# Gate jobs of a two-layer trunk: the eight wide products grouped ahead of the eight narrow ones

## The chip, the cores and the metric

The kernel runs on one core of one Trainium2 chip. A core has a matrix engine, TensorE (PE in the profile; its weight loads are the row PEld), and VectorE (DVE), ScalarE (ACT), GpSimd (POOL) and SyncE (SP, which here only starts transfers). Each works through its own queue in the order in which the program wrote its instructions, and waits on semaphores for the others. The metric is the device time of one launch in microseconds, as the median of several runs; lower is better.

## The reference

The model is a decoder trunk over 512 tokens of width 1024 with two layers, all in float32. Layer 0 is a gated short convolution, layer 1 a sliding-window attention with sinks. Behind each stands the same feed-forward block, with F = 2816, and this block is what the change touches:

```python
def swiglu(h, w_gate_up, w_down):
    g, u = jnp.split(h @ w_gate_up, 2, axis=-1)
    return (jax.nn.silu(g) * u) @ w_down

ff = swiglu(rmsnorm(h, ffn_pre_norm[l]), ffn_w_gate_up[l], ffn_w_down[l])
h = h + rmsnorm(ff, ffn_post_norm[l])
```

## The kernel before

**Split products.** TensorE multiplies a reduced form of float32 (`fp32r`) here, so each factor is split into a high part and a low rest: ScalarE copies the high part (`whi`, L469 for weights), VectorE subtracts it from the full value (`wlo`, L470). A product is then three products, low by high, high by high and high by low; `mm3` (L190 to L193) issues these three into one accumulator.

**Seven products instead of eight.** The columns of the gate and up matrices beyond the first two pairs of blocks are done in groups. A group `q` (0 to 9 in each layer, so 20 in all) takes a 2 by 2 arrangement of weight blocks and of token blocks and forms seven block products, p = 1 to 7, from sums of weight blocks and of token blocks, in place of eight plain ones. Token sums are made once per layer (`factors`, L364), weight sums by accumulating transfers that GpSimd starts (L538) or by VectorE (L457).

**One gate job per product.** `gate_jobs` (L976) makes seven jobs per group in the order p = 1, 2, 6, 5, 7, 3, 4. Jobs 1, 6, 7 and 4 accumulate into chain X, two PSUM tiles `gx` (one for each e = 0, 1); jobs 5 and 3 into chain Z (`gz`), job 2 into chain Y (`gy`). Each job has e = 0, 1 and k = 0 to 3, so eight steps. Jobs 1, 2, 3 and 5 call `mm3` in each step: three products with 256 moving columns, 24 per job. For p = 6, 7 and 4 the token factor lies in one tile with its high and low halves, and a view of it with two stretches of 256 columns (`two[:, :, c:c+256]`, L387) is moved at once. So each step of jobs 6, 7 and 4 is one wide product of 512 columns, `whi` by both halves into the whole tile `gx` (L1048), and one narrow product of 256 columns, `wlo` by the high half into the first 256 columns of the same tile (L1050). There are 3 x 20 = 60 such jobs, and in each the wide and narrow products alternate: wide, narrow, wide, narrow, sixteen in all. In all three jobs the tile is already open, job 1 having started it.

**What follows a job.** `take(p)` (L1001) moves partial sums out of PSUM directly behind each job: for p = 6 and 4 a ScalarE copy (L1024) and a VectorE addition (L1008) for e = 0, then the same for e = 1; for p = 7 two VectorE additions for each e. The next X job may write `gx` only when these have read it; between two X jobs always lies a Y or Z job, except between job 4 of one group and job 1 of the next, which has other tiles.

**The order of work.** The code is under `tc.manual_schedule`: the order on each engine is the order in which the Python code emits instructions. `in_line` (L474) walks over the jobs of a layer: it emits a job's products, then the split of the weights for the job three places ahead (L500), further transfers and pending late steps. Between groups stand the down jobs, which multiply the gated activations by the down matrix with 512 moving columns (`seven`, L604, and `mm3`, tiles `px`, `py`, `pz`). A job's `whi` and `wlo` come from four buffers each, so the split for the job three ahead reuses the buffer of the job just before the current one.

Of the kernel before, what the change touches and what calls it, by code (L numbers as in the profile page):

```python
# [16 lines left out]
P = 128  # L17
D = 1024
S = 512
# [53 lines left out]
def yoco_kernel(  # L73
# [22 lines left out]
    nc = tc.nc  # L96
# [19 lines left out]
    def slot(s, dt=F32, w=S):  # L116
        return big.tile([P, w], dt, tag="slot", name=name(s), padded_shape=[P, S])

    def wide(s, dt=F32):
        return wides.tile([P, D], dt, tag="wide", name=name(s))  # L120
# [7 lines left out]
    def bank(s, pool=None):  # L128

        if pool is None:  # L130
            pool = (ps_mm, ps_sc, ps_mm, ps_pt)[turn[0] % 4]
            turn[0] += 1
        return pool.tile([P, S], F32, tag="bank", name=name(s))
# [56 lines left out]
    def mm3(out, whi, wlo, xhi, xlo, start, stop, **kw):  # L190
        nc.tensor.matmul(out, whi, xlo, start=start, stop=False, **kw)  # L191
        nc.tensor.matmul(out, whi, xhi, start=False, stop=False, **kw)  # L192
        nc.tensor.matmul(out, wlo, xhi, start=False, stop=stop, **kw)  # L193
# [354 lines left out]
    for l in range(2):  # L548
# [3 lines left out]
        for rd, (f0, f1) in enumerate(ROUNDS[:-1]):  # L552
            k = slice(f0 // 2, f1 // 2)
# [106 lines left out]
    with tc.manual_schedule(engines=ALL):  # L660
# [25 lines left out]
        for k in range(KT):  # L686
# [7 lines left out]
            for i in range(3):  # L694
                for t in range(3):
                    n = 3 * k + t
                    whi, wlo = (w[:, n % KT * P : (n % KT + 1) * P] for w in ws[n // KT])
                    nc.tensor.matmul(begun[0][t], (whi, wlo, whi)[i], xs[k][i == 2],
                                     start=k == i == 0, stop=k == KT - 1 and i == 2)
# [255 lines left out]
    def ffn(l, before, ahead, gain, gpres, following):  # L955
# [20 lines left out]
        def gate_jobs(q, factors, out, to, then):  # L976

            sums = sums_of[f"g{l}{q}"]  # L980
            a21, a22, a11, a12 = (Raw(b) for b in sums.blocks)
            s1, s3, *rest = (Raw(b) for b in sums.sums)
            raws = {1: [a11], 2: [a12], 5: [s1], 7: [s3], 4: [a22]}
            if rest:
                raws[6], raws[3] = ([r] for r in rest)
            else:
                raws[6], raws[3] = [a11, s1], [a12, a11]
            chain = {1: "X", 6: "X", 7: "X", 4: "X", 5: "Z", 3: "Z", 2: "Y"}
            pools = {"X": ps_mm, "Y": ps_pt, "Z": ps_sc}
            split = {}  # L990
            if q == 0:

                pools = {"X": ps_sc, "Y": ps_pt, "Z": ps_mm}
                raws[1], raws[2] = [], []
                split = {1: ahead.ready[4], 2: ahead.ready[5]}
            banks, kept = {}, []

            def tiles(a):
                return a.rearrange("p (e c) -> p e c", e=2)

            def take(p):  # L1001
                x, y, z = (banks.get(c) for c in "XYZ")
                st, u, gr = kept
                g0, g1 = (gr.rearrange("p (e h c) -> p e h c", e=2, h=2)[:, :, h]
                          for h in range(2))

                def add(out, a, b):
                    nc.vector.tensor_tensor(out=out, in0=a, in1=b, op=ALU.add)  # L1008

                if p == 2:  # L1010
                    add(g0, tiles(y), tiles(st))
                elif p == 5:
                    nc.scalar.activation(u, z, AF.Copy)
                elif p == 3:
                    add(g1, tiles(z), tiles(st))
                else:
                    for e in range(2):
                        a, b = x[e][:, :256], x[e][:, 256:]
                        ste, ue = (v[:, e * 256 : (e + 1) * 256] for v in (st, u))
                        if p == 7:  # L1020
                            add(ue, a, ue)
                            add(ue, b, ue)
                            continue
                        nc.scalar.activation(ste, a, AF.Copy)  # L1024
                        if p != 1:
                            add(ste, b, ste)
                if p == 4:
                    for g, m in ((g0, st), (g1, u)):
                        nc.vector.scalar_tensor_tensor(out=g, in0=tiles(m), scalar=-1.0, in1=g,
                                                       op0=ALU.mult, op1=ALU.mult)  # L1030

            def run(p):
                def products(job):
                    if not kept:
                        kept.extend([slot("st"), slot("st"), wide("gr")])
                    whi, wlo = split[p] if p in split else job.w
                    c = chain[p]
                    opened = c not in banks
                    if opened:
                        banks[c] = ([bank("gx", pools[c]) for _ in range(2)] if c == "X"  # L1040
                                    else bank("g" + c.lower(), pools[c]))
                    for e in range(2):
                        for k in range(4):
                            kk = slice(e * S + k * P, e * S + (k + 1) * P)
                            xhi, xlo, *xboth = factors[p][k]
                            kw = {"skip_group_check": True}
                            if c == "X" and xboth:
                                nc.tensor.matmul(banks[c][e], whi[:, kk], xboth[0], start=False,  # L1048
                                                 stop=False, **kw)
                                nc.tensor.matmul(banks[c][e][:, :256], wlo[:, kk], xhi,  # L1050
                                                 start=False, stop=k == 3 and p == 4, **kw)
                                continue
                            out = (banks[c][e][:, :256] if c == "X"
                                   else banks[c][:, e * 256 : (e + 1) * 256])
                            mm3(out, whi[:, kk], wlo[:, kk], xhi, xlo,
                                opened and k == 0 and (c == "X" or e == 0),
                                e == 1 and k == 3 and p in (2, 3), **kw)
                    take(p)
                return products

            def gate():
                nc.scalar.activation(kept[2], kept[2], AF.Silu)  # L1062

            def end():
                late = out(kept[2], to)
                then()
                return late

            return [Job(raws[p], run(p), {3: gate, 4: end}.get(p), len(raws[p]) > 1)
                    for p in (1, 2, 6, 5, 7, 3, 4)]  # L1070
# [42 lines left out]
        with tc.manual_schedule(engines=ALL):  # L1113
# [5 lines left out]
            def then(hf, k):  # L1119
                if hf == 0 and k in (5, 6):  # L1120
                    for b in ((0, 1), (2, 3))[k - 5]:
                        before.turn(b, (2,))
                if hf == 0 and k == 6:
                    for b in range(4):
                        before.turn(b, (3,))
                    for f in range(KT):
                        before.split(0, f, 1)
                    for b in range(4):
                        before.keep(b, 1)
                if hf == 1 and k == 1:  # L1130
                    factors.update(before.factors())
                if hf == 1 and k == 3:
                    sum_on(f"{l}f0")

            factors = {}
# [137 lines left out]
    class Heads:  # L1273
# [114 lines left out]
        def out(self):  # L1388
            hi, lo = slot("ohi", F32R), slot("olo", F32R)
            nc.scalar.activation(hi, self.po, AF.Copy)  # L1390
            nc.vector.tensor_tensor(out=lo, in0=self.po, in1=hi.bitcast(F32), op=ALU.subtract)
            at.append((hi, lo))
# [25 lines left out]
    with tc.manual_schedule(engines=ALL):  # L1418
        last_tile(res, [[(0, 4)], [(0, 5)], [], [(0, 6), (0, 7), (1, 0), (1, 1)],
                        [(1, f) for f in (4, 5, 2, 3, 6, 7)]])  # L1420
        for hf in range(2):
            c = slice(hf * 256, (hf + 1) * 256)
            for k in range(KT):
                kk = slice(k * P, (k + 1) * P)
# [192 lines left out]
```

## Time and profile before

| quantity | value |
|---|---|
| median of 3 runs | 1027.26 us (1026.03 to 1027.35) |
| time of the profiled execution | 1026.46 us |
| its span, first to last instruction | 1024.7 us |
| TensorE busy / weight loads busy | 1015.1 us / 900.3 us |
| VectorE / ScalarE / GpSimd busy | 858.7 / 582.3 / 196.9 us |
| granted TensorE clock | 0.999 |
| wide products of the 60 jobs (L1048) | 480, mean 399 ns |
| narrow products of the 60 jobs (L1050) | 480, mean 281 ns |

Products are pipelined: the duration of one is longer than the distance from its start to the start of the next, and durations overlap. What a sequence of products costs is therefore read from start times in the timeline, not from durations. The two feed-forward blocks' gate and down jobs run from 203.9 us to 470.9 us and from 709.3 us to 975.9 us of the span.

### The profile page before, as it was taken

The page shows a single profiled execution, that of the slowest core. Times are in us where ns is not written, and L with a number is a line of the kernel's source. Part 1 is how long each engine was busy: PE and PEld are TensorE (multiplying, and loading weights), DVE is VectorE, ACT ScalarE, POOL GpSimd, SP SyncE. Part 2 cuts the span into 40 slices and gives each one's busy share as a digit, 9 for nine tenths or more (in the row PEclk, how much of TensorE's full clock was granted, in tenths as well). Part 3 has the DMA queues.
Part 4 walks back from the last instruction along what each step waited for, and adds up shares of the span by engine and source line. Part 5 has one row for each costly group of instructions (what it writes and reads, how often), then busy time and mean ns, then how long its engine had stood idle before and what let it go on. Part 6 is the DMA issues. An engine that isn't in the chain of part 4 may idle for free.

```text
span 1024.7 us, 16538 instructions
## 1 busy us (share of the span) xinstructions
PE 1015.1 (99%) x6168; PEld 900.3 (88%) x6168; DVE 858.7 (84%) x1440; ACT 582.3 (57%) x1035; POOL 196.9 (19%) x259
## 2 busy tenths in 40 slices
PE   9999999999999999999999999999999999999997
PEld 8888888999889898998897888889998998989986
DVE  5766767889789988989869998778997898889896
ACT  7323445865655454666476776677666554645641
POOL 0443033112111111000123653232111010110001
PEclk9999999999999999999999999999999999999999
DMA  9897689459979699879504779976899576998742
GB/s 357 288 266 225 184 255 350 136 167 292 348 238 296 195 305 307 267 210 318 170 5 160 187 229 277 254 264 153 270 289 328 167 245 226 299 298 249 240 149 82
DMA packets 66576, 244.52 MB, mean 239 GB/s; under 512 B 7872, under 2 KB 8384, under 8 KB 54720
## 3 DMA queue, kind: packets, MB, share of 16 engines
q1 hardware_dynamic: 51328, 145.98, 38.9%
q0 software_dynamic: 14592, 96.48, 36.9%
q8 instruction: 48, 0.79, 0.3%
q10 hardware_dynamic: 576, 1.02, 0.3%
q14 instruction: 32, 0.26, 0.1%
HBM read 237.15 MB, written 102.76 MB: 332 GB/s over the span
## 4 chain that ended last, share of the span: by engine, by line
PE 85%; DVE 8%; ACT 2%; DMA 2%; issue 2%; POOL 0%; DVEq 0%; ACTq 0%
PE gx L1048 10%; PE gx L1050 5%; PE pcub L191 4%; PE pcub L192 4%; PE pcub L193 4%; PE gz L193 3%; PE gz L192 3%; PE gz L191 3%; PE px L191 3%; PE px L193 3%; PE px L192 3%; PE pmix L191 2%; PE pmix L192 2%; PE pmix L193 2%; DMA raw<-in_w_gb_dram 2%; PE gy L193 2%
## 5 line engine op out<-in xcount | busy, mean ns | idle before, releaser
L470 DVE TENSOR_TENSOR wlo<-raw,whi 128x1024 fp32r<-128x1024 f32 x225 | 274.8, 1227 | 64.5 <-ACT whi L469 64.1
L469 ACT ACTIVATE whi<-raw 128x1024 fp32r<-128x1024 f32 x225 | 234.0, 1051 | 104.8 <-DVE raw L457 22.3
L1048 PE MATMUL gx<-xt,whi 128*128 128x512 f32 x480 | 172.5, 399 | 0.1
L1050 PE MATMUL gx<-xt,wlo 128*128 128x256 f32 x480 | 135.0, 281 | 0.0
L1048 PEld LDWEIGHTS gx<-xt,whi 128*128 128x128 f32 x480 | 90.4, 188 | 19.7 <-DVE st L1008 0.3
L538 POOL DMA_DIRECT2D hsum<-in_w_gb_dram x96 | 63.7, 751 | 143.9 <-ACT whi L469 82.6
L1050 PEld LDWEIGHTS gx<-xt,wlo 128*128 128x128 f32 x480 | 90.9, 189 | 0.1
L1024 ACT ACTIVATE st<-gx 128x256 f32<-128x256 f32 x120 | 43.0, 379 | 63.1 <-PE gx L1050 47.8
L538 POOL DMA_DIRECT2D hsum<-hsum x32 | 25.3, 790 | 258.9 <-ACT whi L469 192.0
L1008 DVE TENSOR_TENSOR st<-gx,st 128x256 f32<-128x256 f32 x160 | 62.9, 420 | 4.3 <-ACT st L1024 2.9
L192 PE MATMUL pcub<-xhi,whi 128*128 128x512 f32 x168 | 65.4, 389 | 0.0
L191 PE MATMUL pcub<-xlo,whi 128*128 128x512 f32 x168 | 65.4, 389 | 0.0
L193 PE MATMUL pcub<-xhi,wlo 128*128 128x512 f32 x168 | 65.4, 389 | 0.0
L1062 ACT ACTIVATE gr<-gr 128x1024 f32<-128x1024 f32 x20 | 21.3, 1065 | 49.2 <-DVE gr L1008 49.2
L191 PE MATMUL px<-wlo,ahi 128*128 128x512 f32 x120 | 46.8, 390 | 0.1
L192 PE MATMUL px<-whi,ahi 128*128 128x512 f32 x120 | 46.7, 389 | 0.0
L193 PE MATMUL px<-whi,alo 128*128 128x512 f32 x120 | 46.7, 389 | 0.0
L193 PE MATMUL gz<-xhi,wlo 128*128 128x256 f32 x160 | 45.4, 284 | 0.0
L191 PE MATMUL gy<-xlo,whi 128*128 128x256 f32 x160 | 45.3, 283 | 0.0
L192 PE MATMUL gy<-xhi,whi 128*128 128x256 f32 x160 | 45.3, 283 | 0.0
L193 PE MATMUL gy<-xhi,wlo 128*128 128x256 f32 x160 | 45.3, 283 | 0.0
L192 PE MATMUL gx<-xhi,whi 128*128 128x256 f32 x160 | 45.3, 283 | 0.0
(265 smaller groups left out, 3064.5 us busy)
## 6 DMA issues: line engine op xcount, KB each, us to landing
hsum<-in_w_gb_dram POOLq DMA_DIRECT2D x96, 512.0 KB, 7.9
raw<-hsum SPq DMA_DIRECT2D x88, 512.0 KB, 7.6
raw<-in_w_gb_dram SPq DMA_DIRECT2D x60, 512.0 KB, 7.6
hsum<-in_w_dn_dram POOLq DMA_DIRECT2D x36, 512.0 KB, 8.8
raw<-in_w_dn_dram SPq DMA_DIRECT2D x32, 512.0 KB, 6.0
hsum<-hsum POOLq DMA_DIRECT2D x28, 512.0 KB, 5.9
raw<-in_w_in_dram SPq DMA_DIRECT2D x21, 512.0 KB, 7.8
hsum<-in_w_dn_dram POOLq DMA_DIRECT2D x12, 768.0 KB, 12.8
```

Source lines behind the costliest of these rows:

```text
L191: nc.tensor.matmul(out, whi, xlo, start=start, stop=False, **kw)
L192: nc.tensor.matmul(out, whi, xhi, start=False, stop=False, **kw)
L193: nc.tensor.matmul(out, wlo, xhi, start=False, stop=stop, **kw)
L469: self.begun = nc.scalar.activation(hi[:, :n], raw, AF.Copy)
L470: nc.vector.tensor_tensor(out=lo[:, :n], in0=raw, in1=hi[:, :n].bitcast(F32), op=ALU.subtract)
L538: nc.gpsimd.dma_start(dst, src, max_dma_last_dim=4 * 4 * S, **kw))
L1008: nc.vector.tensor_tensor(out=out, in0=a, in1=b, op=ALU.add)
L1024: nc.scalar.activation(ste, a, AF.Copy)
L1048: nc.tensor.matmul(banks[c][e], whi[:, kk], xboth[0], start=False, stop=False, **kw)
L1050: nc.tensor.matmul(banks[c][e][:, :256], wlo[:, kk], xhi, start=False, stop=k == 3 and p == 4, **kw)
L1062: nc.scalar.activation(kept[2], kept[2], AF.Silu)
```

## The change

In `run(p)` of `gate_jobs`, the eight steps (e, k) become a list. For the jobs that have the two-half token view (p = 6, 7 and 4) the kernel now issues the eight wide products in the order of the list first, and then the eight narrow products in the same order. Number, operands and shapes of the instructions are the same as before. The wide products get `start=opened and k == 0` in place of `start=False`; since chain X is already open in these jobs, this is the same value. The other jobs issue what they did.

```diff
-                    for e in range(2):
-                        for k in range(4):
-                            kk = slice(e * S + k * P, e * S + (k + 1) * P)
-                            xhi, xlo, *xboth = factors[p][k]
-                            kw = {"skip_group_check": True}
-                            if c == "X" and xboth:
-                                nc.tensor.matmul(banks[c][e], whi[:, kk], xboth[0], start=False,
-                                                 stop=False, **kw)
-                                nc.tensor.matmul(banks[c][e][:, :256], wlo[:, kk], xhi,
-                                                 start=False, stop=k == 3 and p == 4, **kw)
-                                continue
+                    steps = [(e, k, slice(e * S + k * P, e * S + (k + 1) * P))
+                             for e in range(2) for k in range(4)]
+                    kw = {"skip_group_check": True}
+                    if c == "X" and len(factors[p][0]) == 3:
+                        for e, k, kk in steps:
+                            nc.tensor.matmul(banks[c][e], whi[:, kk], factors[p][k][2],
+                                             start=opened and k == 0, stop=False, **kw)
+                        for e, k, kk in steps:
+                            nc.tensor.matmul(banks[c][e][:, :256], wlo[:, kk], factors[p][k][0],
+                                             start=False, stop=k == 3 and p == 4, **kw)
+                    else:
+                        for e, k, kk in steps:
                             out = (banks[c][e][:, :256] if c == "X"
                                    else banks[c][:, e * 256 : (e + 1) * 256])
-                            mm3(out, whi[:, kk], wlo[:, kk], xhi, xlo,
+                            mm3(out, whi[:, kk], wlo[:, kk], *factors[p][k][:2],
                                 opened and k == 0 and (c == "X" or e == 0),
                                 e == 1 and k == 3 and p in (2, 3), **kw)
                     take(p)
```

## The prediction

> **What bounds the kernel now.** I read the page's engine table first, then the busy times of one feed-forward block, and then the timeline of TensorE product by product, since only start times tell what a pipelined product costs.
>
> ```profile
> PE 1015.1 (99%) x6168; PEld 900.3 (88%) x6168; DVE 858.7 (84%) x1440; ACT 582.3 (57%) x1035; POOL 196.9 (19%) x259
> ```
>
> ```profile
> 709.30:975.90 266.60, 266.60 (x1735) 243.88 (x1734) 234.33 (x339) 155.11 (x227) 30.36 (x46) 1.00 0.81 257
> ```
>
> The reader is to see that TensorE is busy for 99% of the span and that in the second block's stretch (columns: length, then busy time of PE, PEld, DVE, ACT and POOL, granted clock, DMA share) it has no idle time at all: 266.60 of 266.60 us, at full clock, with DVE at 234.33. So in the stretch that the change touches the end is set by how closely TensorE's products follow each other. A wait that is shortened elsewhere buys nothing there; a product that starts sooner does.
>
> **What is touched.** The groups by line give the number of products:
>
> ```profile
> L1048 PE MATMUL gx<-xt,whi 128*128 128x512 f32 x480 | 172.5, 399 | 0.1
> L1050 PE MATMUL gx<-xt,wlo 128*128 128x256 f32 x480 | 135.0, 281 | 0.0
> ```
>
> 480 of each at 8 per job are 60 jobs. Nothing is added or removed: the same 960 products and weight loads, no DMA, no instruction on another engine, and no queue is passed by another step. Only TensorE's order changes, and with it the moments at which `whi`, `wlo` and the two `gx` tiles are first needed or finished.
>
> **What the alternating order costs.** One job of before (start, duration, then the product):
>
> ```profile
> 206.82 0.28 PE L191 MATMUL gy<-xlo,whi 128*128 128x256 f32 x1
> ...
> 209.70 0.40 PE L1048 MATMUL gx<-xt,whi 128*128 128x512 f32 x1
> 209.94 0.28 PE L1050 MATMUL gx<-xt,wlo 128*128 128x256 f32 x1
> 210.05 0.40 PE L1048 MATMUL gx<-xt,whi 128*128 128x512 f32 x1
> 210.29 0.28 PE L1050 MATMUL gx<-xt,wlo 128*128 128x256 f32 x1
> ...
> 212.53 0.28 PE L191 MATMUL gz<-xt,whi 128*128 128x256 f32 x1
> ```
>
> The 24 narrow products of `gy` run from 206.82 to 209.70: 2.88 us, 0.120 each. The sixteen of the job run from 209.70 to 212.53: 2.83 us, 0.354 for a wide and narrow pair. What would eight wide in a row cost? Here is a steady row of wide products (six distances):
>
> ```profile
> 59.74 0.39 PE L191 MATMUL pcub<-xlo,whi 128*128 128x512 f32 x1
> ...
> 61.10 0.39 PE L191 MATMUL pcub<-xlo,whi 128*128 128x512 f32 x1
> ```
>
> 1.36 / 6 = 0.227 each. A steady wide and a steady narrow one are 0.347 together, so the alternating pair pays 0.007 more. The row just after a change of width is not steady, though. Two places where wide products follow a row of narrow ones:
>
> ```profile
> 539.49 0.28 PE L193 MATMUL pv<-whi,xlo 128*128 128x256 f32 x1
> 539.61 0.40 PE L191 MATMUL pq<-xlo,whi 128*128 128x512 f32 x1
> 539.84 0.40 PE L192 MATMUL pq<-xhi,whi 128*128 128x512 f32 x1
> ...
> 541.45 0.39 PE L193 MATMUL pq<-xhi,wlo 128*128 128x512 f32 x1
> ```
>
> ```profile
> 660.98 0.40 PE L191 MATMUL pmix<-wlo,ohi 128*128 128x512 f32 x1
> ...
> 662.82 0.39 PE L193 MATMUL pmix<-whi,olo 128*128 128x512 f32 x1
> ```
>
> In both, eight distances take 1.84 us, 0.23 each: 0.03 over the steady 8 x 0.227 = 1.81. The first distance is 0.23 (539.61 to 539.84), about what the first wide product of a gate job shows (209.70 to 209.94). These wide products read 512 adjoining columns and those of L1048 two stretches of 256; the first distance gives no sign that the two stretches cost anything by themselves. The way back, narrow after wide:
>
> ```profile
> 292.29 0.39 PE L193 MATMUL px<-whi,alo 128*128 128x512 f32 x1
> 292.52 0.28 PE L191 MATMUL gx<-xlo,whi 128*128 128x256 f32 x1
> 292.63 0.28 PE L192 MATMUL gx<-xhi,whi 128*128 128x256 f32 x1
> ...
> 293.47 0.28 PE L193 MATMUL gx<-xhi,wlo 128*128 128x256 f32 x1
> ```
>
> Eight distances from 292.52 to 293.47 are 0.95 us, the first of them 0.11. So I read the 0.007 as the price of never settling: each change of width disturbs the spacing, a row of equal products settles after a few, an alternating row cannot.
>
> **The sum.** A new job is 1.84 + 0.95 = 2.79 us. Three such jobs and the two Z jobs between them, 24 narrow products each, run from the first wide product of job 6 to the first product of the next group:
>
> ```profile
> 229.70 0.40 PE L1048 MATMUL gx<-xt,whi 128*128 128x512 f32 x1
> ...
> 243.95 0.28 PE L191 MATMUL gx<-xlo,whi 128*128 128x256 f32 x1
> ```
>
> Before: 14.25 us. After: 3 x 2.79 + 2 x 2.88 = 14.13. That is -0.12 a group and -2.4 us over 20 groups. Starts are rounded to 0.01, so a group's gain is between 0.08 and 0.16, and the whole between -1.6 and -3.2 us.
>
> Given back, first, where a down job follows job 4 (4 groups of each layer, 8 in all). After the alternating row its wide products settle at once, and after narrow ones they will not:
>
> ```profile
> 263.95 0.40 PE L191 MATMUL px<-wlo,a 128*128 128x512 f32 x1
> ...
> 265.77 0.39 PE L193 MATMUL px<-whi,a 128*128 128x512 f32 x1
> ```
>
> Eight distances are 1.82 there against the 1.84 above: 8 x 0.02 = +0.2 us.
>
> Second, the one place where TensorE waits inside a gate job for more than its weights' order, group 7 of the first block:
>
> ```profile
> 421.94 0.28 PE L193 MATMUL gz<-xt,wlo 128*128 128x256 f32 x1
> 422.36 0.50 PE L1048 MATMUL gx<-xt,whi 128*128 128x512 f32 x1
> ```
>
> ```profile
> 389.37 18.78 DMA raw<-in_w_gb_dram
> ```
>
> The start of L1048 is 0.42 after its forerunner in place of 0.12. The chain of waits leads back to a weight transfer of 18.78 us that was issued at 389.37. What TensorE gains while that transfer is under way is lost at this wait; what it gained before moves the issue forward too, since the transfer waits for a buffer that TensorE's pace sets free. Bounds: nothing lost, or all that groups 0 to 6 gained, 7 x 0.12 = 0.84 us. I take 0.2, near the lower end, as less than two groups lie inside the transfer. The second block has no such wait (266.60 of 266.60).
>
> The waits of the other engines. For p = 6 the copy of e = 0 waits for TensorE, and so does that of e = 1:
>
> ```profile
> 231.36 0.39 ACT L1024 ACTIVATE st<-gx 128x256 f32<-128x256 f32 x1 [1.75 <-PE gx L1050]
> 232.80 0.39 ACT L1024 ACTIVATE st<-gx 128x256 f32<-128x256 f32 x1 [1.05 <-PE gx L1050]
> ```
>
> Tile e = 0 is now finished at 1.84 + 4 x 0.12 = 2.32 us into the job in place of half of 2.83, so 0.9 later, and the first copy moves by that, to 232.26; it ends at 232.65, still ahead of the second copy at 232.80. What ScalarE does next stands behind both and does not move. For p = 7 VectorE starts at its own time:
>
> ```profile
> 238.93 1.67 DVE L1008 TENSOR_TENSOR st<-gx,st 128x256 f32<-128x256 f32 x4
> ```
>
> The job began at 235.41 (5.71 after 229.70: a job and a Z job), so the four additions start 3.52 into it, after both tiles are finished in either order. They end at 240.60, and the next X job begins at 241.12, another 5.71 on and 0.52 later; its first write to tile e = 1 comes after four wide products (0.92) in place of four pairs (1.42), still behind 240.60. So these edits cost 0, and the cover is 0.52 us for e = 0. `wlo` is needed 1.84 into the job in place of 0.23; as TensorE hardly ever waits, I give that nothing.
>
> Sum: -2.4 + 0.2 + 0.2 = -2.0 us. Against the profiled execution's 1026.46 us (span 1024.7) that is 1024.5. The median of the runs shown, 1027.26, is 0.8 above that execution, so I forecast 1025.3 for the median. 0.2% of this kernel is 2.05 us, about what a measurement can tell from no change; the forecast lies on that border.
>
> **Rivals.** First, no effect of the order: each product costs what its own shape costs, and the 0.007 belongs to the two-stretch read of L1048. Then a wide one is 0.354 - 0.120 = 0.234 wherever it stands, a new job is 8 x 0.354 = 2.83 as before, and the time stays at 1027.3. For it: no trace row has two-stretch wide products in a row. Against it: the first distances of both kinds of wide products agree, and adjoining ones pay the same 0.23 while they settle. The Trainium skill, "TensorE: Matmul & The Clock Gate", section "Back-to-back issue gap", gives each product a gap by its own column count alone, columns / 2.4 + 2.5 ns, which says the same: regrouping moves nothing. The trace does not agree with that page in full: it shows 0.227 and 0.120 where the page's formula gives 0.216 and 0.109, and a pair that is more than the sum of its two.
>
> Second, slower: the two-stretch read costs more than 0.234 and the narrow product behind it hides a part, since narrow ones follow at 0.11 in the alternating row (209.94 to 210.05). In a row of wide ones it would show in full. At 0.24 each, the largest distance in the alternating rows (210.05 to 210.29), a job is 8 x 0.24 + 0.95 = 2.87, 0.04 more, 60 x 0.04 = +2.4 us: 1029.7. It decides from 0.235 a wide product on, and passes 0.2% at 0.239.
>
> Third, faster still: wide products of these jobs are steady from the first on: 1.81 + 0.95 = 2.76, 60 x -0.07 = -4.2 us: 1023.1. The rows at 539.61 and 660.98 speak against it.
>
> **How the numbers follow.** Settling order effect 0.64, no effect of the order 0.15, slower 0.15, steady at once 0.06. The first case spans -1.2 us to -2.8 (-1.6 and -3.2, with 0.4 given back); of its 0.64 I put 0.37 over the 2.05 us, somewhat more than half, as the loss at the one wait may be nothing. Faster: 0.37 + 0.06 = 0.43. Same: 0.27 + 0.15 - 0.02 for a small loss = 0.40. Slower: 0.15 + 0.02 = 0.17. The likeliest case alone is 1024.5 to 1026.1. The range for 8 in 10 runs from 1023.3, near the steady case, to 1028.0, past no change by the 0.7 us by which the runs shown differ among each other, without the slower case's far end.
>
> **What would show it.** Right: within jobs 6, 7 and 4 the timeline has eight L1048 at 0.23, settling to 0.227, then eight L1050 at 0.12, a job of 2.79 us; a group from job 6 on 14.13 us; the second block about 1.1 us shorter than 266.60. Wrong: L1048 distances that stay at 0.234 or more, or new idle time of TensorE ahead of L1048 with DVE L1008 or ACT L1024 as releaser, which would mean that the 0.52 us of cover is gone; or block times that shrink while the attention part behind them grows.

## The result and the profile after

The changed kernel takes 1024.91 us in the median of 21 runs (1024.04 to 1026.32), the kernel before 1026.27 us in the same comparison (21 runs, 1025.71 to 1028.87). The ratio is 0.9985 with a 95% interval of 0.9978 to 0.9992: faster, by about 1.5 us, which is less than the 0.2% (2.05 us) that the prediction names as the border. The forecast was 1025.3 us, in the range 1023.3 to 1028.0.

The profiled execution took 1026.32 us with a span of 1024.5 us, the slowest of the 21. One must not compare its span with the 1024.7 us of before and conclude that nothing was gained; where it lost time again is shown below. The page of the changed kernel, its engine table and the groups of the wide products (now L1047) and the narrow ones:

```profile
PE 1013.4 (99%) x6168; PEld 900.5 (88%) x6168; DVE 858.7 (84%) x1440; ACT 581.2 (57%) x1035; POOL 196.7 (19%) x259
...
L1047 PE MATMUL gx<-xt,whi 128*128 128x512 f32 x480 | 120.3, 392 | 0.3 <-DVE st L1008 0.3
...
L1050 PE MATMUL gx<-xt,wlo 128*128 128x256 f32 x480 | 66.9, 282 | 0.0
```

The mean durations, 392 and 282 ns, are those of before (399 and 281) within a few ns. The fall of the groups' busy time, from 172.5 and 135.0 us to 120.3 and 66.9, is no gain either: it is the time that a group's own products cover, and in a row they overlap each other instead of the other group. Only starts tell. The timeline of one job of the changed kernel, and the first product of the next group:

```profile
229.47 2.00 PE L1047 MATMUL gx<-xt,whi 128*128 128x512 f32 x8
231.31 1.11 PE L1050 MATMUL gx<-xt,wlo 128*128 128x256 f32 x8
232.26 0.28 PE L191 MATMUL gz<-xt,whi 128*128 128x256 f32 x1
...
243.60 0.28 PE L191 MATMUL gx<-xlo,whi 128*128 128x256 f32 x1
```

The wide row takes 231.31 - 229.47 = 1.84 us, the narrow row 0.95, the job 2.79 where it was 2.83. From job 6 of a group to the next group: 243.60 - 229.47 = 14.13 us where it was 14.25. Now the busy times of the two feed-forward blocks, each from its first gate product to the first product behind its last one, in the changed kernel (length, then busy time of PE, PEld, DVE, ACT and POOL, clock, DMA share, GB/s):

```profile
203.81:469.85 266.04, 265.98 (x1737) 244.13 (x1735) 234.57 (x339) 155.27 (x229) 32.87 (x50) 1.00 0.84 266
707.80:976.08 268.28, 266.79 (x1737) 244.20 (x1735) 234.44 (x339) 154.96 (x229) 30.27 (x46) 1.00 0.82 256
```

and in the kernel before, cut in the same way:

```profile
203.94:471.27 267.33, 267.16 (x1737) 243.94 (x1735) 234.35 (x339) 155.33 (x228) 32.97 (x50) 1.00 0.84 264
709.30:976.23 266.93, 266.91 (x1736) 243.90 (x1735) 234.52 (x339) 155.44 (x228) 30.36 (x46) 1.00 0.81 257
```

The undisturbed blocks are 266.93 us before (the second) and 266.04 after (the first): 0.89 us gained. The first block of before is 0.40 longer than its second; that is the wait at 422.36 us. The second block of after is 2.24 us longer than its first. The timeline of TensorE and the chain of waits of the changed kernel say where:

```profile
913.59 0.39 PE L193 MATMUL px<-whi,alo 128*128 128x512 f32 x1
914.37 0.39 PE L191 MATMUL gx<-xlo,whi 128*128 128x256 f32 x1 [0.40 <-ACT whi L469]
914.59 0.28 PE L192 MATMUL gx<-xhi,whi 128*128 128x256 f32 x1
915.63 0.39 PE L193 MATMUL gx<-xhi,wlo 128*128 128x256 f32 x1 [0.76 <-DVE wlo L470]
...
926.80 0.28 PE L193 MATMUL gz<-xt,wlo 128*128 128x256 f32 x1
927.36 1.42 PE L1047 MATMUL gx<-xt,whi 128*128 128x512 f32 x5 [0.28 <-DVE st L1008]
```

```profile
892.63 20.53 DMA raw<-in_w_gb_dram
...
913.26 1.07 ACT whi L469
```

A weight transfer issued at 892.63 us takes 20.53 us; the weights' split (L469) can begin at 913.26 only, and TensorE stands still for the high part, then for the low part, and once more behind VectorE's late additions. By the starts shown the three come 0.55, 0.92 and 0.44 us later than the usual 0.23 or 0.12 behind their forerunners: 1.9 of the 2.24 us. It is the same pair of transfers, in the same place behind group 6 of a layer, as the one that stopped the kernel before at 422.36 us, in the other block.

### The profile page after: what moved, and what is told of

It reads as the page before. It is cut to its first block, busy times and chain, and to the rows that moved or that the text cites. A ratio compares the mean times of both kernels' runs of the same rounds, so it can differ in the third digit from the quotient of the medians.

```text
span 1024.5 us, 16538 instructions
## 1 busy us (share of the span) xinstructions
PE 1013.4 (99%) x6168; PEld 900.5 (88%) x6168; DVE 858.7 (84%) x1440; ACT 581.2 (57%) x1035; POOL 196.7 (19%) x259
## 4 chain that ended last, share of the span: by engine, by line
PE 85%; DVE 8%; DMA 3%; ACT 2%; issue 2%; POOL 0%; DVEq 0%; SPq 0%; ACTq 0%
PE gx L1047 10%; PE gx L1050 5%; PE pcub L192 4%; PE pcub L193 4%; PE pcub L191 4%; PE gz L193 3%; PE gz L192 3%; PE gz L191 3%; PE px L191 3%; PE px L192 3%; PE px L193 3%; PE pmix L192 2%; PE pmix L191 2%; PE pmix L193 2%; DMA raw<-in_w_gb_dram 2%; PE gy L193 2%
## 5 line engine op out<-in xcount | busy, mean ns | idle before, releaser
L469 ACT ACTIVATE whi<-raw 128x1024 fp32r<-128x1024 f32 x225 | 233.6, 1051 | 106.9 <-DVE raw L457 24.4
L1047 PE MATMUL gx<-xt,whi 128*128 128x512 f32 x480 | 120.3, 392 | 0.3 <-DVE st L1008 0.3
L1047 PEld LDWEIGHTS gx<-xt,whi 128*128 128x128 f32 x480 | 86.3, 189 | 15.9 <-DVE st L1008 0.5
L1050 PEld LDWEIGHTS gx<-xt,wlo 128*128 128x128 f32 x480 | 65.5, 190 | 4.7
L1050 PE MATMUL gx<-xt,wlo 128*128 128x256 f32 x480 | 66.9, 282 | 0.0
L1008 DVE TENSOR_TENSOR st<-gx,st 128x256 f32<-128x256 f32 x160 | 62.7, 419 | 3.4 <-ACT st L1024 1.6
L193 PE MATMUL gx<-xhi,wlo 128*128 128x256 f32 x160 | 45.4, 284 | 0.8 <-DVE wlo L470 0.8
L191 PE MATMUL gx<-xlo,whi 128*128 128x256 f32 x160 | 45.4, 283 | 0.4 <-ACT whi L469 0.4
L192 PE MATMUL gz<-xhi,whi 128*128 128x256 f32 x160 | 45.3, 283 | 0.0
```

Of the source, the lines that this page charges most:

```text
L469: self.begun = nc.scalar.activation(hi[:, :n], raw, AF.Copy)
L1047: nc.tensor.matmul(banks[c][e], whi[:, kk], factors[p][k][2], start=opened and k == 0, stop=False, **kw)
L1050: nc.tensor.matmul(banks[c][e][:, :256], wlo[:, kk], factors[p][k][0], start=False, stop=k == 3 and p == 4, **kw)
```

## The experiments

**Theory and rivals.** Theory: the order alone sets the spacing; a row of equal products settles, an alternating row does not. Rivals: the two-stretch read of the wide products is what costs; or the gain comes from needing `wlo` later in the job. And for the time that is missing: the late transfer belongs to single executions, or the new order brings it.

**Adjoining columns, order of before.** The view with two stretches becomes one of 512 adjoining columns.

```diff
+                    whole = two[:, :S]
-                    made[p] += [[hi[:, c : c + 256], lo[:, c : c + 256], two[:, :, c : c + 256]]
+                    made[p] += [[hi[:, c : c + 256], lo[:, c : c + 256], whole]
```

> Leaves part of the computation out: the wide products of jobs 6, 7 and 4 read 512 adjoining columns of one token tile instead of two stretches of 256, in the alternating order of before. Settling theory (the order sets the spacing, the shape of the read does not): a job from its first wide product to the first product behind it stays at 2.83 us, with distances of 0.23 to 0.24 behind a wide product. Rival (the read of two stretches costs 0.007 by itself): 8 x 0.347 = 2.77 us, and the time falls by about 60 x 0.06 = 3.6 us.

The timeline of this kernel:

```profile
229.56 0.40 PE L1049 MATMUL gx<-xt,whi 128*128 128x512 f32 x1
229.80 0.28 PE L1051 MATMUL gx<-xt,wlo 128*128 128x256 f32 x1
229.91 0.40 PE L1049 MATMUL gx<-xt,whi 128*128 128x512 f32 x1
230.16 0.28 PE L1051 MATMUL gx<-xt,wlo 128*128 128x256 f32 x1
...
232.40 0.28 PE L191 MATMUL gz<-xt,whi 128*128 128x256 f32 x1
```

The job is 2.84 by these rounded starts (2.83 in the median of the 60 jobs), the distances behind a wide product 0.24 and 0.25 as before, the blocks 266.94 and 266.93 us; one run took 1025.82 us, beside a median of 1025.97 for the kernel before. The shape of the read costs nothing that the trace shows. The first rival falls.

**Narrow products first.** The two loops of the change are exchanged, so `wlo` is needed at the job's first product.

```diff
                         for e, k, kk in steps:
-                            nc.tensor.matmul(banks[c][e], whi[:, kk], factors[p][k][2], ...
+                            nc.tensor.matmul(banks[c][e][:, :256], wlo[:, kk], factors[p][k][0], ...
                         for e, k, kk in steps:
-                            nc.tensor.matmul(banks[c][e][:, :256], wlo[:, kk], factors[p][k][0], ...
+                            nc.tensor.matmul(banks[c][e], whi[:, kk], factors[p][k][2], ...
```

> Eight narrow products first, then eight wide ones; the low weight parts are needed at once. Settling theory: 8 x 0.120 + 1.84 = 2.80 us a job, and 0.01 less in the narrow row behind it, so the time is that of the changed kernel, 1.4 us under before (ratio 0.9985), within 0.3 us. Rival (the gain comes from the low weight parts being needed later): the time is that of before.

```profile
203.78:469.75 265.97, 265.97 (x1736) 244.07 (x1735) 234.37 (x339) 155.48 (x228) 32.86 (x50) 1.00 0.83 266
707.67:973.65 265.98, 265.98 (x1736) 244.07 (x1735) 234.43 (x339) 155.37 (x228) 30.27 (x46) 1.00 0.82 257
```

A job takes 2.80 us (229.44 to 232.24 in its timeline), as the theory has it. The blocks are 265.97 and 265.98 us, level with the changed kernel's 266.04, and the ratio to before is 0.9984 (0.9974 to 0.9993), that of the change. The second rival falls too: nothing was gained by the later need of the low parts. Nor was there a wait in the kernel before that a later need could have shortened: its second block has 0.02 us without TensorE work (266.91 of 266.93 us), and here it is 0.95 us shorter.

**Fours.** Four wide, four narrow, twice.

```diff
+                        for at in range(0, 8, 4):
-                        for e, k, kk in steps:
+                            for e, k, kk in steps[at : at + 4]:
                             ... (wide)
-                        for e, k, kk in steps:
+                            for e, k, kk in steps[at : at + 4]:
                             ... (narrow)
```

> Four wide, four narrow, four wide, four narrow. Settling theory, with the first four distances of a wide row (0.233, 0.236, 0.228, 0.232) and of a narrow row (0.113, 0.119, 0.120, 0.120): 2 x 1.40 = 2.80 us a job, between the 2.79 of eight and the 2.83 of one. Rival (what the change gained comes from needing the low weight parts later, not from the spacing): jobs that do not wait keep 2.83.

```profile
229.43 1.09 PE L1048 MATMUL gx<-xt,whi 128*128 128x512 f32 x4
230.36 0.63 PE L1051 MATMUL gx<-xt,wlo 128*128 128x256 f32 x4
230.84 1.09 PE L1048 MATMUL gx<-xt,whi 128*128 128x512 f32 x4
231.76 0.64 PE L1051 MATMUL gx<-xt,wlo 128*128 128x256 f32 x4
232.24 0.28 PE L191 MATMUL gz<-xt,whi 128*128 128x256 f32 x1
```

2.81 us a job, blocks of 266.41 us: between before and after, as the theory has it (2.80); the rival had 2.83. One run took 1024.75 us.

**Twos.** The same loop with steps of two.

```diff
-                        for at in range(0, 8, 4):
+                        for at in range(0, 8, 2):
```

> Two wide, two narrow, four times. Settling theory: 4 x (0.233 + 0.236 + 0.116 + 0.120) = 2.82 us a job. Rival (a fixed price for each change of width, taken from 2.83 with eight changes to narrow and 2.79 with one): 2.79 + 3 x 0.0056 = 2.81 us.

```profile
230.10 0.63 PE L1048 MATMUL gx<-xt,whi 128*128 128x512 f32 x2
230.57 0.39 PE L1051 MATMUL gx<-xt,wlo 128*128 128x256 f32 x2
230.80 0.63 PE L1048 MATMUL gx<-xt,whi 128*128 128x512 f32 x2
...
232.89 0.28 PE L191 MATMUL gz<-xt,whi 128*128 128x256 f32 x1
```

2.79 us a job, and both blocks 265.85 us: shorter than with rows of eight; one run took 1024.31 us. Here the theory in the form of the prediction falls, which had 2.82, and so does the fixed price for each change of width, 2.81. With four changes to narrow the job pays less than fours with two, and two wide and two narrow products take 0.697 (2.787 / 4), 0.003 over twice the steady 0.347, though no row in it is long enough to settle.

**Threes, and one by one with the narrow product first.** Rows of three, three and two; and a loop over the steps that issues the narrow product, then the wide one.

```diff
-                        for at in range(0, 8, 4):
+                        for at in range(0, 8, 3):
```

> Rows of three: three wide, three narrow, twice, then two and two. The runs so far gave 2.832, 2.787, 2.807 and 2.793 us a job for rows of one, two, four and eight. If the price goes by the number of changes of width alone, three must lie between two and four, 2.79 to 2.81. [...]

```diff
                         for e, k, kk in steps:
+                            nc.tensor.matmul(banks[c][e][:, :256], wlo[:, kk], ...
+                            nc.tensor.matmul(banks[c][e], whi[:, kk], ...
```

> Narrow, wide, narrow, wide, eight times: rows of one, begun by the narrow product. If alternating one by one is what costs, whichever begins, a job and the first products behind it take 2.83 us as before and the time is that of before. If the beginning sets it, the job differs from 2.83 by more than 0.01.

The second block of the threes and of the narrow-first alternation:

```profile
707.51:973.35 265.84, 265.79 (x1737) 243.56 (x1735) 234.28 (x339) 155.38 (x229) 30.30 (x46) 1.00 0.81 259
```

```profile
709.13:976.17 267.04, 267.04 (x1736) 243.96 (x1735) 234.64 (x339) 155.18 (x228) 30.30 (x46) 1.00 0.81 257
```

The threes took 1023.59 us in their one run, the alternation 1026.46, the kernel before 1025.64 in one run beside them. Alternating one by one is what costs, whichever product begins: 267.04 us a block and 2.83 us a job (median of the 60 jobs). Lengths of a block by the length of the rows: one 266.93, two 265.85, three 265.84, four 266.41, eight 266.04. So neither the number of changes of width nor a settling time gives the order of these five; rows of four are worse than rows of two and of eight. The job alone does not give it either: a job of threes takes 2.797 us, inside the 2.79 to 2.81 that was expected if the number of changes alone set the price, and more than the 2.787 of twos, but the 24 narrow products behind it take 2.869 us in place of 2.880 (medians of the starts in the traces), so the order inside a job also sets the row behind it. What decides between the lengths stays open. No run varies the weight load that goes with every product, so whether it takes part is not shown.

**The changed kernel again.** No edit.

> The changed kernel once more, unaltered. Theory on the missing part (waits for one late weight transfer around 390 to 430 us and 890 to 930 us come and go from run to run; they are no part of the change): a profile whose two blocks are each 266.0 us, or longer by just the idle time of TensorE in these stretches; time 1024.3 to 1025.5. Rival (the change itself brings the wait in the second block): the second block is again over 268 us.

```profile
203.70:469.73 266.03, 265.98 (x1736) 244.18 (x1735) 234.58 (x339) 155.25 (x229) 32.90 (x50) 1.00 0.84 265
707.67:973.71 266.04, 265.99 (x1737) 244.18 (x1735) 234.64 (x339) 155.28 (x229) 30.29 (x46) 1.00 0.81 258
```

Both blocks 266.03 and 266.04, TensorE waits for no late weights, span 1022.2 us, 1023.94 us for this execution. So the changed order does not bring the 2.24 us of the first profile each time. The place is tight in this one too; the longest wait of ScalarE from 885 to 930 us ends with the same transfer (engine and line, released by: us in total, times, longest):

```profile
ACT whi L469 <- DMA raw<-in_w_gb_dram: 4.0, 1, 4.0
```

Here it did not reach TensorE. Of the nine profiles of the study without the edit that follows, two show TensorE losing time at this transfer: the kernel before (first block) and the first profile of the changed kernel (second block). Ten runs gave a median of 1024.56 us (1023.90 to 1026.25), ratio 0.9988 (0.9978 to 0.9997).

**The sums for the last down round one group earlier.** In `BEGIN`, which names the places at which the accumulating transfers of GpSimd begin, once in the changed kernel and once in the kernel before:

```diff
-    ... "0s1": "g09", "0p5": "d03",
+    ... "0s1": "g09", "0p4": "d03",
-    ... "1s1": "g19", "1p5": "d13",
+    ... "1s1": "g19", "1p4": "d13",
```

> The changed kernel, with the sums for the last down round begun one gate group earlier in each layer (after group 4 in place of 5), which moves their transfers away from the late weight transfer. If these sums are what delays it, no waits of TensorE at 390 to 430 and 890 to 930 us in any run, so times nearer together and a median 0.3 to 0.6 us under the changed kernel's, 1024.2. If not, the median and its spread stay; if the sums now collide elsewhere, new waits show and it is slower.

> The kernel before with the same move of the sums. If late transfers cost the two kernels alike, it gains 0.2 to 0.5 us as the changed kernel does, and stays 1.5 to 2.0 us above it. If the changed order is what makes TensorE run into the late transfer, it gains nothing.

The changed kernel with it: median 1024.03 us (1023.78 to 1024.66), ratio to before 0.9978 (0.9969 to 0.9988). The kernel before with it: 1026.36 us (1025.65 to 1026.74), ratio 0.9999 (0.9990 to 1.0009), beside 1026.09 (1025.63 to 1028.07) without. In neither profile does TensorE wait there; the second block of each:

```profile
708.40:974.44 266.04, 265.99 (x1737) 244.17 (x1735) 234.57 (x339) 155.64 (x229) 30.30 (x46) 1.00 0.82 258
```

```profile
709.31:976.23 266.92, 266.92 (x1736) 243.91 (x1735) 234.46 (x339) 155.64 (x228) 30.30 (x46) 1.00 0.81 257
```

The waits of ScalarE from 885 to 930 us, in the changed kernel with the move, now have other releasers:

```profile
ACT whi L469 <- DVE raw L457: 4.7, 1, 4.7
...
ACT whi L469 <- DMA raw<-hsum: 1.3, 2, 1.0
```

The row of the weight transfer `raw<-in_w_gb_dram` is gone, from 385 to 425 us as well, where it stood with 7.5 us in the second profile of the changed kernel. It stands in at least one of these two stretches in all nine profiles without the move and in neither in the three with it, so beginning these sums later is what made ScalarE wait for that transfer; by which route the sums delay it is not shown. ScalarE still waits there, now 4.7 us for VectorE.

What the move is worth in time is less sure: the slowest runs are gone from both kernels (1026.25 became 1024.66, and 1028.07 among 31 runs became 1026.74 among 10), but the medians move by 0.5 us down and 0.3 us up, and the intervals of the ratios overlap those without the move. The kernel before gained nothing, which was expected to mean that the changed order is what makes TensorE run into the late transfer; it stands 2.3 us above the changed kernel with the same move, where 1.5 to 2.0 had been expected. But the kernel before had lost only 0.40 us there, in one of the three profiles with alternating products and without the move, which is little beside its spread, so these runs don't settle whether the new order made TensorE more apt to run into it. One part of the spread the move does not touch: in these two profiles the first gate job starts at 204.47 and 204.42 us, in the changed kernel's second profile at 203.70, without any edit ahead of it.

**Twos and earlier sums together.** Both edits in one kernel.

> Two wide, two narrow, four times, with the sums begun earlier. From the 2.787 us a job that the profile of the twos showed, against 2.793 for eight and eight: 0.2 to 0.4 us a launch under the changed kernel with the same sums, so about 1023.9 and a ratio to before of 0.998. A rival, that the twos gain nothing in time: level with the eights.

Median 1024.03 us (1023.65 to 1024.33), ratio 0.9977 (0.9968 to 0.9986), blocks of 265.85 us. It beats the kernel before by 0.23% (0.14% to 0.32%) and is level with the eights with earlier sums (1024.03), as the rival had it: the 0.4 us that the twos save in the blocks' rows are less than these runs can tell.

## Why the prediction was right, point by point

- **What bounds the kernel.** Right. In the blocks TensorE has 0.05 us of idle time in 266.03 (the second profile of the changed kernel), and the time followed its spacing. The part between the blocks did not grow: 238.03 us before (471.27 to 709.30), 237.94 after (469.73 to 707.67).
- **A new job of 1.84 + 0.95 = 2.79 us, a group of 14.13.** Right to the rounding: 1.84, 0.95 and 14.13 were measured.
- **-2.4 us for the 20 groups.** Too large, inside its own bounds of -1.6 to -3.2. By the unrounded starts in the traces a group went from 14.245 to 14.140 us in the median, 0.105 where the rounded starts gave 0.12, and the 20 groups together became 1.96 us shorter (kernel before with earlier sums against the second profile of the changed kernel, four blocks without a wait).
- **+0.2 us for the down jobs.** About right: the eight distances went from 1.822 to 1.841 us in six of the eight, +0.11 in all; the last down job of each layer shows no such step. The sum left out that the 24 narrow products of the job behind job 4 also take 2.880 us in place of 2.875, +0.06 over the twelve places. Together this gives -1.8, which is what the undisturbed blocks show: 266.04 - 266.93 = -0.89 us each, where about -1.1 was forecast.
- **0.2 us lost at the late transfer, in the first block.** The mechanism is there, its place and size are not fixed: 0.40 us in the first block of before, 2.24 us in the second block of one execution of after, none in either block of the other. In the first block, for which the sum gave back 0.2 us, neither profile of the changed kernel lost anything. The sentence that the second block has no such wait held only for that profile.
- **The waits of ScalarE and VectorE cost nothing.** Right: in the second profile of after TensorE waits for no engine in either block, although e = 0 is finished 0.9 us later. In the first profile it waits once for L1008 (0.28 us), behind the late transfer.
- **"Never settling" as the reason.** In part. That alternating one by one pays more than rows of eight was shown, and that it is the order and not the read; and a row of eight wide products does settle (distances of 0.233, 0.236, 0.228, 0.232, 0.231, then 0.227, medians of the unrounded starts). As a rule it is wrong: rows of two and three, too short to settle, pay less than rows of four and of eight.
- **The rivals.** That the order has no effect and the read costs the 0.007 fell with the changed kernel's job of 2.79 us and with the adjoining columns, which kept the 2.83 us. A dearer read in a row fell with the eight wide products of the changed kernel, 1.84 us or 0.23 each. Steady from the first product on (2.76 us) did not occur. The formula that the first rival cites from the Trainium skill, "TensorE: Matmul & The Clock Gate", section "Back-to-back issue gap", is given there for an isolated product; for a stream of weight loads and products the section says that both set the spacing, so the prediction read it too widely. A gap by the column count alone does not agree with the traces: the same sixteen products with the same weights took 2.83, 2.81 or 2.79 us by their order alone.

The sum came out at -2.0 us, the measured gain at -1.4 between the medians and about -1.5 by the ratio, while the undisturbed blocks hold -1.8. That the forecast of 1025.3 us came within 0.4 of the measured 1024.91 is in part luck: it started from a median of 1027.26, which is 1.0 above the 1026.27 of the 21 runs, and took off 0.6 too much. The case with the highest chance, faster by more than 0.2% (0.43), did not come: the gain stayed under that border.

## What to carry to other kernels

Where TensorE has no idle time, read the spacing of starts for each neighbourhood of shapes and not only per shape: here a wide and a narrow product in turn paid 0.007 us a pair, and grouping them by two, three or eight took most of that back within the job, and the rows behind it took up to 0.02 us each longer or shorter. So price a row together with its neighbours, from a place in the trace where the same change of shape already occurs; that gave 2.79 us a job before the kernel was built. When one profile shows the expected gain in one block and not in the other, look for a wait that comes and goes before doubting the gain, and profile again.

## What the runs showed that was not expected

Rows of two (265.85 us a block) and three (265.84) are shorter than rows of eight (266.04) and of four (266.41); two wide and two narrow products take 0.697 us, 0.003 over their steady distances, while alternating singles take 0.007 over in half as many. The runs give no rule for which length fits. And the weight transfer behind group 6 of a layer took 18.78 us where TensorE lost 0.4 us and 20.53 where it lost 2.2; in the other block of each of these two profiles, and in a second execution of the changed kernel, the same transfer cost TensorE nothing.
